# A two-layer decoder trunk: probabilities and last residual turned over by pass-through transposes, rows normalized first, tiles at multiples of 64 bytes

## The chip, the cores and the metric

The kernel runs on one core of a Trainium2 chip. The metric is the device time of one execution in microseconds (us). Every time below comes from the profile page of the kernel before, from queries to its trace, or from the list of its runs.

## What is computed

Batch 1, 512 tokens, model width 1024, two layers, float32 throughout. Layer 0 mixes tokens with a chunked gated MLP, layer 1 with forgetting attention; each is followed by a convolutional gated MLP (FFN), and a last RMSNorm ends the trunk. The part of the reference that the change touches is the softmax and its product with the values, and the last residual addition:

```python
logits = logits + cum[:, :, q0:q1, None] - cum[:, :, None, :q1]
logits = jnp.where(mask, logits, neg)
p = jax.nn.softmax(logits, axis=-1)
outs.append(jnp.einsum("bhqk,bkhd->bqhd", p.astype(vb.dtype), vb))
...
h = h + conv_gated_ffn(hn, ...)      # the last one, then
return rmsnorm(h, final_norm_g)
```

There are 16 heads of 64 features and four query blocks of 128 tokens; query block qi sees (qi + 1) * 128 keys.

## The kernel before, in words

All large products are made on TensorE from operands split into two float32r parts (hi and lo), as three products for one (`triple`, lines 164 to 169). Weights arrive as 176 units of 128x1024 (`raw`), are split by ScalarE (`whi`, line 112) and VectorE (`wlo`, line 113) and feed either `gemm_fm` (weights stationary, 512 tokens moving) or `gemm_tm` (tokens stationary, 512 weight columns moving). Activations that enter from a norm lie in tiles `x`; those that enter an output or down projection lie in tiles `z`. So the products with `z` are the gMLP's output projection (8 output tiles x 16 k tiles x 3 = 384 products of 512 columns), the first FFN's down projection (384), the attention's output projection (8 x 8 x 3 = 192) and the last down projection `last_down`, where `z` is the stationary side (7 token tiles of 512 columns over two groups x 16 x 3 = 336, and one tile in two halves of 256 columns, 96).

Where a tile lies is settled by the order in which its name is first asked for. The tile `mv` (line 227, statistics of the layer norm) takes 128 x (4 x 2) floats, 32 bytes of a partition. The tiles asked for before it and used on TensorE (`h`, `raw`, `whi`, `wlo`, `x`, `tmp`, `ident`, `v`) begin at multiples of 64 bytes; `R`, `pt`, `tc`, `z` and `hl`, asked for after it, begin 32 bytes beyond one.

The attention runs in slots of `attend` (line 518): a slot issues the sums of values of a block that is 7 slots old, then the transposes (`turn`) of one that is 5 slots old, then the logits of a new one. Blocks of the q and k projections (`qk`, two heads a time, 16 blocks of 3 products) are put between slots by a list written out by hand, `(4, 2, 2, 2, 2, 2, 1, 1)` blocks ahead of the 8 slots of two heads. For the last pair of heads, blocks of the output projection take their place. The engines run beside one another, each in an order fixed when the program is built.

`logits(h, qi)` makes two products into PSUM (lines 542 and 543) and adds the mask (544). VectorE takes the negated row maximum (546), ScalarE the exponentials with their sum into the head's tile `pr` (tag `pt`, line 547), VectorE the inverse of the sum (548), and then a 128x128 diagonal of the inverses in a tile `dg` (tag `tmp`, line 549). `turn(h, kb)` multiplies each 128x128 block of `pr`, as the stationary side, by the diagonal of its query block (line 559), which transposes and normalizes at once; there are 4 + 3 + 2 + 1 = 10 such products a head. They are plain float32 products, and the trace shows each as two records, a weight load and a matmul in both. The result is split (lines 112 and 113 into `hl`) and multiplied with the values (572 and 573).

`last_down` puts the residual into PSUM ahead of the down projection: 32 products of a 128x128 block of `h`, as the stationary side, with the identity (line 634), 16 ahead of each of the two groups.

Of the kernel before, what the change touches and what calls it, by code (L numbers as in the profile page):

```python
# [12 lines left out]
AF = mybir.ActivationFunctionType  # L13
ALU = mybir.AluOpType
# [3 lines left out]
T = 512            # tokens  # L18
D = 1024
KD = D // P        # feature tiles of the model width  # L20
E = 2048           # gMLP width and FFN width
KE = E // P
G = 8              # spatial groups
NT = T // P        # token tiles
H = 16             # heads
# [4 lines left out]
LAG = 7            # blocks between the logits and the sums of values  # L30

# columns of the packed per-feature vectors
V_MIX = 0          # mix_norm_g, 2 layers x 8 tiles
V_FFN = 16         # ffn_norm_g, 2 x 8
V_CW = 32          # conv taps, 2 x 3 x 16
V_CB = 128         # conv bias, 2 x 16
V_LG = 160         # ln_g, 16
V_LB = 176         # ln_b, 16
NV = 192
NU = 176           # units of weights  # L40


class Trunk:
# [41 lines left out]
    def unit(self):  # L85
        """The next unit of weights, in two parts; the one after it is under way."""
        while len(self.ahead) < 2 and self.iu < NU - 4:
            self.fetch()
        return self.ahead.pop(0)

# [1 line left out]
    def rsqrt(self, src, n, scale, eps):  # L92
        """[P, n] -> 1/sqrt(src*scale + eps): a first guess from the exponent, then Newton."""
        nc = self.nc
        ms, y, t = self.small(n), self.small(n), self.small(n)
        nc.vector.tensor_scalar(out=ms, in0=src, scalar1=scale, scalar2=eps, op0=ALU.mult, op1=ALU.add)
        nc.vector.tensor_scalar(out=y.bitcast(I32), in0=ms.bitcast(I32), scalar1=-0.5, scalar2=float(0x5F3759DF),
                                op0=ALU.mult, op1=ALU.add)
        for _ in range(3):
            self.newton(y, ms, t)  # L100
        return y

    def newton(self, y, ms, t):
        """y towards 1/sqrt(ms)."""
        nc = self.nc
        nc.vector.tensor_tensor(out=t, in0=y, in1=y, op=ALU.mult)
        nc.vector.scalar_tensor_tensor(out=t, in0=t, scalar=-0.5, in1=ms, op0=ALU.mult, op1=ALU.mult)
        nc.vector.scalar_tensor_tensor(out=y, in0=t, scalar=1.5, in1=y, op0=ALU.add, op1=ALU.mult)
# [6 lines left out]
    def norm_split(self, k, gcol, parts=1):  # L115
        """Operand parts of h*g for feature tile k."""
        nc = self.nc
        if k == 0:
            self.acc, self.xh, self.xl = None, [], []
        h = self.h[k]  # L120
        g = self.vec[:, gcol + k : gcol + k + 1]
        xh = self.sb("x", 16, [P, T], F32R)
        xl = self.sb("x", 16, [P, T], F32R)
        for q in range(parts):
            c = slice(q * T // parts, (q + 1) * T // parts)
            nc.scalar.activation(out=xh[:, c], in_=h[:, c], func=AF.Copy, scale=g)
            nc.vector.scalar_tensor_tensor(out=xl[:, c], in0=h[:, c], scalar=g, in1=xh[:, c].bitcast(F32),
                                           op0=ALU.mult, op1=ALU.subtract)
        self.xh.append(xh)
        self.xl.append(xl)  # L130

    def norm_square(self, k):
        """Feature tile k's share of the sum of squares."""
        nc = self.nc
        if self.acc is None:
            self.acc = self.tmp()
            nc.scalar.activation(out=self.acc, in_=self.h[k], func=AF.Square)
        else:
            sq = self.tmp()
            nc.scalar.activation(out=sq, in_=self.h[k], func=AF.Square)  # L140
            nc.gpsimd.tensor_tensor(out=self.acc, in0=self.acc, in1=sq, op=ALU.add)  # L141

    def norm_end(self):
        """r4[:, i]: 1/rms of token i*128+p.  R: the same along the free axis, on every partition."""
        nc = self.nc
        pt = self.ps("a")
        for i in range(NT):
            nc.tensor.matmul(pt[:, i : i + 1], self.acc[:, i * P : (i + 1) * P], self.ones[:, 0:1], start=True, stop=True)
        self.r4 = self.rsqrt(pt[:, 0:NT], NT, 1.0 / D, RMS_EPS)
        dg = self.tmp()  # L150
        for i in range(NT):
            nc.vector.tensor_scalar(out=dg[:, i * P : (i + 1) * P], in0=self.ident, scalar1=self.r4[:, i : i + 1],
                                    scalar2=None, op0=ALU.mult)
        self.dg = dg
# [9 lines left out]
    def triple(self, out, a, b, start, stop):  # L164
        """a*b to float32's accuracy from the exact parts of a and b."""
# [5 lines left out]
    def gemm_fm(self, o, nk, groups, evac, each=None, banks0=None):  # L171
        """Feature-major: four 128-feature tiles a group, weights stationary.  Yields after every 128x128 block."""
# [15 lines left out]
    def gemm_tm(self, o, nk, groups, evac, each=None):  # L188
        """Token-major: four token tiles a group of 512 features, tokens stationary."""
# [21 lines left out]
    def add_to_h(self, gcol):  # L211
        """Evacuation of an output product: the residual, then the next norm's operand."""
# [10 lines left out]
    def gmlp(self):  # L223
# [3 lines left out]
        mv = self.sb("mv", 1, [P, NT, 2])  # L227
# [38 lines left out]
        def mix(c):  # L266
            """The mixed chunks of feature tile c, with the norm's scale and shift and the spatial bias."""
# [42 lines left out]
    def spatial(self):  # L310
        """Causal spatial weights, transposed: [s, g, t], with their sums over s on every partition."""
# [46 lines left out]
    def fox(self):  # L358
# [4 lines left out]
        # the parts of the gates' weights side by side  # L363
# [44 lines left out]
        # Blocks of products fill the tensor engine's waits in the attention: logits of one head beside  # L408
        # the transposes and sums of the one before it.
# [20 lines left out]
    def gates(self):  # L430
        """Logs of the forget gates, [token, head]."""
# [14 lines left out]
        # log sigmoid z = min(z, 0) - log(1 + e^-|z|);  log(1 + e^-|z|) = 2 atanh s,  s = (1 - th)/(3 + th),  th = tanh(|z|/2)  # L446
# [15 lines left out]
    def running_sums(self):  # L462
        """Running sums of the logs, [head, token], in two parts, and negated: four rows a head beside the parts of
        q and of k: cum, cum, 1, 1 and 1, 1, -cum, -cum."""
# [29 lines left out]
    def stack_q(self, p, pq, st):  # L494
        """Operands of the logits of heads 2p and 2p+1: the parts of q and k, stacked along the contraction."""
# [22 lines left out]
    def attend(self, slot):  # L518
        """Logits of one block; some blocks behind them the transposes, and behind those the sums of values."""
# [9 lines left out]
    OFF = (0, 128, 384, 768)   # where the rows of a query block begin in a head's tile of probabilities  # L529

    def logits(self, h, qi):
        """Softmax's numerators of query block qi, and the diagonal of its normalizers' inverses."""
        nc = self.nc
        if qi == 0:
            self.pr[h] = (self.sb("pt", 3, [P, 1280]), self.tmp())
        pr, dg = self.pr[h]
# [10 lines left out]
        nc.scalar.activation(out=pr[:, self.OFF[qi] : self.OFF[qi] + w], in_=s[:, 0:w], func=AF.Exp, bias=nm, accum_out=sm)  # L547
        nc.vector.reciprocal(out=rc, in_=sm)
        nc.vector.tensor_scalar(out=dg[:, q], in0=self.ident, scalar1=rc, scalar2=None, op0=ALU.mult)

    def turn(self, h, kb):
        """Probabilities of key block kb, transposed and normalized, in two parts."""
        nc = self.nc
        pr, dg = self.pr[h]
        n = (NT - kb) * P
        pt = self.ps("a")
        for qi in range(kb, NT):
            o = self.OFF[qi] + kb * P
            nc.tensor.matmul(pt[:, (qi - kb) * P : (qi - kb + 1) * P], pr[:, o : o + P], dg[:, qi * P : (qi + 1) * P],  # L559
                             start=True, stop=True)  # L560
# [28 lines left out]
    def last_down(self):  # L589
        """Token-major down projection with the residual, then the final norm."""  # L590
# [13 lines left out]
        def finish(i, parts):  # L604
            # 1/rms from a square root and one step of Newton's
# [18 lines left out]
        for g in range(2):  # L624
            # a token tile's columns, in two parts where the norm of the last tile waits for them
# [4 lines left out]
            for i in range(NT):  # L630
                for bank, c in parts[i]:
                    for k in range(c.start // P, c.stop // P):
                        o = k * P - c.start
                        nc.tensor.matmul(bank[:, o : o + P], self.h[4 * g + k][:, i * P : (i + 1) * P], self.ident,  # L634
                                         start=o == 0, stop=False)
# [12 lines left out]
        # the last quarter token tile by token tile, so that only the last tile's norm is left at the end  # L648
# [16 lines left out]
    def build(self):  # L665
        nc, tc = self.nc, self.tc
        with tc.tile_pool(name="sb", bufs=1) as self.pool, \
# [3 lines left out]
            # the activation table and the tensor engine's clock get ready while the first loads run  # L671
# [64 lines left out]
def blocks(w):  # L736
    """[K, 512*n] -> units of two 128-row tiles by 512 columns, group by group."""
# [5 lines left out]
def qk_blocks(w):  # L743
    """q and k columns of a pair of heads beside each other, four 128-row tiles a unit."""
# [49 lines left out]
```

## Time and profile before

| what | us |
|---|---|
| runs: median of 3 (lowest to highest) | 1113.28 (1111.95 to 1115.22) |
| profiled execution: span, first to last instruction | 1110.7 |
| its own time beside the span | not listed apart; the fastest run is 1.25 above the span |
| TensorE matmul busy | 1098.0 (99%) |
| TensorE weight loads busy | 905.7 (82%) |
| VectorE busy | 618.5 (56%) |
| ScalarE busy | 443.5 (40%) |
| TensorE's granted clock, mean | 0.998 |

A matmul's duration in the trace is from its start until its modelled end; matmuls overlap, so the distance from one start to the next is what one costs TensorE. Busy times count overlapping instructions of an engine once. Idle time of an engine that does not set the end costs nothing.

### The profile page before, as it was taken

The numbers are of one execution on the slowest core, as the hardware profiler recorded it, in microseconds if no ns is written. First come the engines' busy times: TensorE is split into PE (matmuls) and PEld (weight loads), VectorE is DVE, ScalarE is ACT, GpSimd is POOL, SyncE is SP. The second block draws the span as 40 slices with busy tenths as digits, with TensorE's granted clock in tenths as the row PEclk, the third lists the DMA queues.
The fourth block names the chain that finished last, engine by engine and source line by source line (L and its number), as shares of the span: only waits on it lengthen the run. The fifth ranks groups of instructions, "written<-read, shape, count | busy, mean of one in ns | idle before, by whom it ended". The sixth has DMA issues, their size and how long they took to land. (4 is left out here: it accounts for less than half of the span.)

```text
span 1110.7 us, 13297 instructions
## 1 busy us (share of the span) xinstructions
PE 1098.0 (99%) x5210; PEld 905.7 (82%) x5210; DVE 618.5 (56%) x1007; ACT 443.5 (40%) x706; POOL 66.4 (6%) x62
## 2 busy tenths in 40 slices
PE   8999999999999999999999999999999999999997
PEld 6878888888888888888888788888878888888886
DVE  6435765533556655624264688888665656644232
ACT  5332333332334333423142566776542434332222
POOL 6000000000200000001020000000021000000000
PEclk9999999999999999999999999999999999999999
DMA  7322222223222222222222212111122222222222
GB/s 245 103 78 98 91 76 95 76 95 95 95 95 95 94 95 95 95 96 94 95 95 82 79 40 62 58 40 58 62 90 95 95 96 95 95 95 94 96 77 76
DMA packets 28959, 99.47 MB, mean 90 GB/s; under 512 B 3488, under 2 KB 4256, under 8 KB 28896
## 3 DMA queue, kind: packets, MB, share of 16 engines
q1 hardware_dynamic: 28752, 98.52, 26.9%
q8 instruction: 41, 0.67, 0.2%
q14 instruction: 22, 0.18, 0.1%
q10 hardware_dynamic: 144, 0.10, 0.0%
HBM read 96.12 MB, written 2.10 MB: 88 GB/s over the span
## 5 line engine op out<-in xcount | busy, mean ns | idle before, releaser
L113 DVE TENSOR_TENSOR wlo<-raw,whi 128x1024 fp32r<-128x1024 f32 (+1 forms) x173 | 218.8, 1266 | 389.8 <-ACT whi L112 377.4
L112 ACT CAST whi<-raw 128x1024 fp32r<-128x1024 f32 (+1 forms) x173 | 180.7, 1045 | 467.0 <-PE psg L168 124.2
L167 PE MATMUL psg<-x,whi 128*128 128x512 f32 x336 | 136.7, 407 | 0.0
L169 PE MATMUL psg<-x,wlo 128*128 128x512 f32 x336 | 131.3, 391 | 0.0
L168 PE MATMUL psg<-x,whi 128*128 128x512 f32 x336 | 130.8, 389 | 0.0
L167 PE MATMUL pss<-x,whi 128*128 128x512 f32 x208 | 81.9, 394 | 0.0
L169 PE MATMUL pss<-x,wlo 128*128 128x512 f32 x208 | 81.0, 390 | 0.0
L168 PE MATMUL pss<-x,whi 128*128 128x512 f32 x208 | 80.9, 389 | 0.0
L169 PEld LDWEIGHTS psg<-x,wlo 128*128 128x128 f32 x336 | 63.1, 188 | 13.8
L167 PEld LDWEIGHTS psg<-x,whi 128*128 128x128 f32 x336 | 63.9, 190 | 11.1 <-issue 0.2
L168 PEld LDWEIGHTS psg<-x,whi 128*128 128x128 f32 x336 | 63.3, 189 | 11.2 <-issue 0.2
L141 POOL TENSOR_TENSOR tmp<-tmp,tmp 128x512 f32<-128x512 f32 x28 | 46.3, 1655 | 408.4 <-ACT tmp L140 406.9
L167 PE MATMUL psg<-z,whi 128*128 128x512 f32 x128 | 51.1, 401 | 0.0
L168 PE MATMUL psg<-z,whi 128*128 128x512 f32 x128 | 50.6, 395 | 0.0
L169 PE MATMUL psg<-z,wlo 128*128 128x512 f32 x128 | 50.6, 395 | 0.0
L559 PE MATMUL psa<-tmp,pt 128*128 128x128 f32 x320 | 47.4, 278 | 0.2 <-DVE hl L113 0.2
L168 PEld LDWEIGHTS pss<-x,whi 128*128 128x128 f32 x208 | 39.1, 188 | 8.2 <-issue 0.2
L169 PEld LDWEIGHTS pss<-x,wlo 128*128 128x128 f32 x208 | 39.0, 188 | 8.2
L547 ACT ACTIVATE pt<-pss,sm 128x128 f32<-128x128 f32 (+1 forms) x64 | 33.7, 527 | 30.1 <-DVE sm L546 29.7
L167 PEld LDWEIGHTS pss<-x,whi 128*128 128x128 f32 x208 | 39.1, 188 | 8.1 <-issue 0.2
L559 PEld LDWEIGHTS psa<-tmp,pt 128*128 128x128 f32 x320 | 43.1, 191 | 2.9 <-DVE hl L113 1.3
L167 PE MATMUL psa<-x,whi 128*128 128x512 f32 x112 | 44.2, 394 | 0.0
(283 smaller groups left out, 2279.2 us busy)
## 6 DMA issues: line engine op xcount, KB each, us to landing
raw<-w SPq DMA_DIRECT2D x175, 512.0 KB
out<-v SPq DMA_DIRECT2D x8, 256.0 KB
h<-x SPq DMA_DIRECT2D x3, 512.0 KB
raw<-w SPq DMA_DIRECT2D x2, 256.0 KB
h<-x SPq DMA_DIRECT2D x4, 128.0 KB
pt<-ws SPq DMA_DIRECT2D x1, 512.0 KB
pt<-bs SPq DMA_DIRECT2D x1, 512.0 KB
z<-cum SPq DMA_DIRECT2D x32, 8.0 KB
```

The costliest lines, as they stand in the source:

```text
L112: nc.scalar.copy(out=hi, in_=src)
L113: nc.vector.tensor_tensor(out=lo, in0=src, in1=hi.bitcast(F32), op=ALU.subtract)
L141: nc.gpsimd.tensor_tensor(out=self.acc, in0=self.acc, in1=sq, op=ALU.add)
L167: self.nc.tensor.matmul(out, ah, bh, start=start, stop=False)
L168: self.nc.tensor.matmul(out, ah, bl, start=False, stop=False)
L169: self.nc.tensor.matmul(out, al, bh, start=False, stop=stop)
L547: nc.scalar.activation(out=pr[:, self.OFF[qi] : self.OFF[qi] + w], in_=s[:, 0:w], func=AF.Exp, bias=nm, accum_out=sm)
L559: nc.tensor.matmul(pt[:, (qi - kb) * P : (qi - kb + 1) * P], pr[:, o : o + P], dg[:, qi * P : (qi + 1) * P], start=True, stop=True)
```

## The change

Four edits. `logits` no longer makes a diagonal; it multiplies the row of `pr` in place by the inverse of its sum, 128 to 512 columns. `turn` transposes each block with `nc.tensor.transpose` (the data pass through TensorE, the identity is the moving side). `last_down` marks its 32 products with the identity as transposes. `mv` is asked for with 64 bytes of a partition, of which half is used, so that all later tiles move by 32 bytes. All other lines of the diff take out comments.

```diff
-        mv = self.sb("mv", 1, [P, NT, 2])
+        mv = self.sb("mv", 1, [P, NT, 4])[:, :, 0:2]
...
         if qi == 0:
-            self.pr[h] = (self.sb("pt", 3, [P, 1280]), self.tmp())
-        pr, dg = self.pr[h]
+            self.pr[h] = self.sb("pt", 3, [P, 1280])
+        pr = self.pr[h]
...
-        nc.scalar.activation(out=pr[:, self.OFF[qi] : self.OFF[qi] + w], in_=s[:, 0:w], func=AF.Exp, bias=nm, accum_out=sm)
+        row = pr[:, self.OFF[qi] : self.OFF[qi] + w]
+        nc.scalar.activation(out=row, in_=s[:, 0:w], func=AF.Exp, bias=nm, accum_out=sm)
         nc.vector.reciprocal(out=rc, in_=sm)
-        nc.vector.tensor_scalar(out=dg[:, q], in0=self.ident, scalar1=rc, scalar2=None, op0=ALU.mult)
+        nc.vector.tensor_scalar(out=row, in0=row, scalar1=rc, scalar2=None, op0=ALU.mult)
...
-        pr, dg = self.pr[h]
+        pr = self.pr[h]
...
-            nc.tensor.matmul(pt[:, (qi - kb) * P : (qi - kb + 1) * P], pr[:, o : o + P], dg[:, qi * P : (qi + 1) * P],
-                             start=True, stop=True)
+            nc.tensor.transpose(pt[:, (qi - kb) * P : (qi - kb + 1) * P], pr[:, o : o + P], self.ident)
...
                         nc.tensor.matmul(bank[:, o : o + P], self.h[4 * g + k][:, i * P : (i + 1) * P], self.ident,
-                                         start=o == 0, stop=False)
+                                         start=o == 0, stop=False, is_transpose=True)
```

## Rows read from the trace of the kernel before

**Rows 1.** The page's first part: busy us (share of span), instructions.
```profile
PE 1098.0 (99%) x5210; PEld 905.7 (82%) x5210; DVE 618.5 (56%) x1007; ACT 443.5 (40%) x706; POOL 66.4 (6%) x62
```

**Rows 2.** TensorE's waits, whole run: its longest, and the one at the transposes.
```profile
PE psg L168 <- DVE wlo L113: 2.3, 2, 1.4
...
PE psa L559 <- DVE hl L113: 0.2, 1, 0.2
```

**Rows 3.** Windows of one pair of heads each: first and last of six.
```profile
core 0: us, PE busy (x) PEld busy (x) DVE busy (x) ACT busy (x) POOL busy (x), PEclk, DMA share, GB/s
640.00:661.54 21.54, 21.54 (x130) 18.38 (x129) 17.93 (x44) 14.94 (x35) 1.67 (x2) 1.00 0.17 51
...
747.70:769.24 21.54, 21.54 (x130) 18.36 (x129) 18.01 (x45) 15.24 (x36) 1.23 (x2) 1.00 0.15 49
```

**Rows 4.** Windows in products of `z` moving, `x` moving, `z` stationary; columns as above.
```profile
210.00:280.00 70.00, 70.00 (x302) 56.22 (x301) 23.06 (x21) 17.18 (x20) 5.33 (x3) 1.00 0.29 96
320.00:460.00 140.00, 140.00 (x619) 115.96 (x618) 82.77 (x107) 53.68 (x67) 0.00 (x0) 1.00 0.29 95
...
1022.00:1054.00 32.00, 32.00 (x139) 25.77 (x138) 8.21 (x8) 7.69 (x10) 0.00 (x0) 1.00 0.28 85
```

**Rows 5.** TensorE's timeline, residual of the last projection: start, us, instruction, records merged.
```profile
1007.20 1.05 PE L634 MATMUL psa<-ident,h 128*128 128x128 f32 x8
1008.09 1.06 PE L634 MATMUL psb<-ident,h 128*128 128x128 f32 x8
1008.98 0.39 PE L634 MATMUL psg<-ident,h 128*128 128x128 f32 x2
```

**Rows 6.** Groups by line: the transposing products of the attention; records, busy us, mean ns.
```profile
L559 PE MATMUL psa<-tmp,pt 128*128 128x128 f32 x320 | 47.4, 278 | 0.2 <-DVE hl L113 0.2
```

**Rows 7.** TensorE's timeline: float32 products that move one column, and their neighbours.
```profile
847.36 0.39 PE L169 MATMUL psb<-x,wlo 128*128 128x512 f32 x1
847.59 0.95 PE L148 MATMUL psa<-ones,tmp 128*128 128x1 f32 x8
848.39 0.49 PE L167 MATMUL pss<-x,whi 128*128 128x512 f32 x1
848.72 0.40 PE L168 MATMUL pss<-x,whi 128*128 128x512 f32 x1
```

**Rows 8.** TensorE's timeline: two float32r products that move 128 columns.
```profile
801.45 0.22 PE L572 MATMUL psb<-hl,v 128*128 128x128 f32 x1
801.50 0.30 PE L573 MATMUL psb<-hl,v 128*128 128x128 f32 x1
801.64 0.44 PE L167 MATMUL psg<-z,whi 128*128 128x512 f32 x1
```

**Rows 9.** VectorE's groups by form: scaling 128 columns by one scalar; 512 by two.
```profile
L549 DVE TENSOR_SCALAR tmp<-ident,sm 128x128 f32<-128x128 f32 x64 | 18.9, 295 | 1.5
L259 DVE TENSOR_SCALAR v<-v,mv,sm 128x512 f32<-128x512 f32 x16 | 7.6, 538 | 0.0
```

**Rows 10.** VectorE's waits from 640 to 770 us: us in total, times, longest.
```profile
DVE sm L548 <- ACT pt L547: 7.9, 13, 0.7
DVE wlo L113 <- ACT whi L112: 4.5, 6, 0.7
```

**Rows 11.** Timelines: a head's last diagonal on VectorE, then its first transposes on TensorE.
```profile
665.59 0.28 DVE L549 TENSOR_SCALAR tmp<-ident,sm 128x128 f32<-128x128 f32 x1
...
666.31 1.06 PE L559 MATMUL psa<-tmp,pt 128*128 128x128 f32 x8
```

**Rows 12.** Groups by form: products of 512 columns with `x` and with `z`.
```profile
L168 PE MATMUL psg<-x,whi 128*128 128x512 f32 x336 | 130.8, 389 | 0.0
...
L168 PE MATMUL psg<-z,whi 128*128 128x512 f32 x128 | 50.6, 395 | 0.0
```

**Rows 13.** ScalarE's exponentials: the group over all forms, and reading out the sums.
```profile
L547 ACT ACTIVATE pt<-pss,sm 128x128 f32<-128x128 f32 (+1 forms) x64 | 33.7, 527 | 30.1 <-DVE sm L546 29.7
...
L547 ACT ACTIVATION_READ_ACCUMULATOR pt<-pss,sm 128x1 f32 x64 | 12.3, 193 | 0.0
```

## The prediction, made before the changed kernel ran

> **What bounds the kernel now.** First the page's busy shares: TensorE works in 99% of the span, VectorE in 56%, ScalarE in 40% [rows 1]. A high share may still hide waits, so next the list of waits: in the whole run TensorE's longest entry is 2.3 us, and at the transposes it waits 0.2 us in all [rows 2]. So TensorE's own work sets the time in every stage, and what leaves TensorE leaves the span, as long as nothing else is late in its place. The place to look for that is the attention. There a window of one pair of heads (two heads, 8 slots) repeats every 21.54 us; TensorE fills it, VectorE works 18.0 of it, ScalarE 15.2 [rows 3]. Only here is a second engine near the bound; in the stages of large products VectorE works 33% (23.06 of 70 us) to 59% (82.77 of 140) [rows 4]. Gains elsewhere can be taken whole, gains here only until VectorE is full.
>
> Durations are those of the profiled execution, whose span is 1110.7 us; the median of the runs, 1113.3, is 2.6 above it (0.2%). I take my sum off the median, as what lies around the span stays.
>
> **Last residual.** Sixteen records follow one another at 8.98 - 7.20 = 1.78 us, 0.111 us each [rows 5]. A product with the identity is two records, 0.223 us. What a pass-through transpose costs is not in the trace. Low end: 0.05 us, the distance between two single-record products of 128 columns [rows 8]. High end: 0.223, if it still runs as two records; nothing makes it less than one pass over the same columns, and a price above is a rival below. The nearest row is that of products which move a single column: eight records in 0.80 us, with a late next matmul (0.33 instead of 0.23) 0.90, so 0.11 a record with next to nothing to move [rows 7]. That is the price of loading a float32 block of 128 columns as weights, and a transpose still loads one. I take one record, 0.111 us. So 32 x 0.111 = **3.6 us** gained (0 to 32 x 0.17 = 5.4). TensorE alone is busy here; nothing covers or eats the gain.
>
> [...]
>
> **Turning the probabilities.** 320 records of the same kind [rows 6] are 160 products, 20 a pair of heads. On TensorE a pair loses 20 x 0.111 = 2.2 us: 21.54 becomes 19.3. VectorE gets more to do. Line 549 costs 295 ns for 128 columns now; 512 columns by two scalars cost 538 [rows 9]. Straight between them, rows of 128, 256, 384 and 512 cost 295, 376, 457 and 538 ns, 0.49 us a head more, 0.97 a pair. VectorE then needs 18.0 + 0.97 = 18.97 us of a pair that TensorE could do in 19.3. It is in order and waits for ScalarE now, 7.9 us for exponentials and 4.5 for weight parts in the 6 pairs from 640 to 770 us, 2.1 a pair [rows 10]. If all of that stayed, a pair would last 21.1 us; if none, 19.3. A fuller VectorE has other work in hand when an exponential is late, so I take a value nearer the TensorE end, 20.1 us. What is late next is the last row of a head: its diagonal is done at 665.87 and the head's transposes begin at 666.31 [rows 11]. The 0.24 us that the row of 512 costs more fits into these 0.44 today, but not with certainty when TensorE comes 10% earlier; behind the waiting transpose stand the logits and projections of the slot. That is why I don't take 19.3.
>
> Seven pairs of 20 make 140 of the 160 transposes. Gain 7 x (21.54 - 20.1) = 10.1 us. The last 20 run beside the output projection with little for VectorE to do: 20 x 0.111 = 2.2. Together **12.3 us**. Bounds: with pairs of 21.1, 3.1 + 2.2 = 5.3; with transposes of 0.05 us TensorE would need 21.54 - 3.4 = 18.1 and VectorE's 18.97 would bind, 7 x 2.57 + 20 x 0.17 = 21.4. The diagonal's tile is no longer held; no wait for a `tmp` tile stands among the waits, so that counts nothing. ScalarE and the queues of DMAs get no instruction more or less.
>
> **Tiles at multiples of 64 bytes.** The matmuls with `x` last 389 ns, those with `z` 395 [rows 12]. What each costs is seen in windows: 302 matmuls touch 70 us of products that move `z`, 139 touch 32 us in which `z` is stationary, 619 touch 140 us of products that move `x` [rows 4]. As a matmul of 0.39 us is counted in both windows at an edge, I take off 1.7: 0.2331, 0.2331 and 0.2268 us. All are at full clock, with the same 128 weight columns and 512 moving columns. `x`, `whi` and `wlo` lie at multiples of 64 bytes, `z` 32 beyond; whichever side `z` is on, the product costs 6.3 ns more. After the change `z` lies as `x` does. 384 + 384 + 192 + 336 = 1296 products of 512 columns with `z`: 1296 x 0.0063 = **8.2 us**. Bounds: 0, if the place matters for another reason; 9, if the 96 half-wide products gain as well. A loss is excluded as far as the trace tells, since the tiles move to where the faster ones are. The logits, values and `pt` blocks move too; a few ns on some 32 products a pair lie within the bounds.
>
> **Sum.** 12.3 + 3.6 + 8.2 = 24.1 us. 1113.3 - 24.1 = **1089 us** (2.2%; span 1086.6).
>
> **Rivals.**
> A: the place of `z` is not the cause. For it: 16 `z` tiles lie in another part of the memory than `x`, and no row separates the place from the remainder by 64. Against: 6.3 ns with `z` on either side, in stages with idle and with busy VectorE. Then 24.1 - 8.2 = 15.9: 1097 us. [...]
> B: VectorE holds the pairs at 21.1 us, as all its waits for ScalarE stay. Gain 5.3 + 3.6 + 8.2 = 17.1: 1096 us.
> C: the change doesn't do what it says: a float32 transpose still takes two records of 0.111 us. VectorE's 18.97 hides in 21.54, and only the 8.2 remain: 1105 us; with A as well 1113, no change.
> D, slower: the order of VectorE puts each inverse right behind its row maximum, so that it stands through every exponential. Eight a pair, 527 + 193 ns each [rows 13], 5.8 us: 18.97 + 5.8 = 24.7 us a pair. That costs 7 x 3.2 = 22.4 against 2.2 + 3.6 + 8.2 = 14.0 gained elsewhere: 1122 us. It decides from pairs of 21.54 + (14.0 + 3.3) / 7 = 24.0 us on. Against: now VectorE does other work between the two, and waits there 13 times in 48 exponentials [rows 10].
> [...]
>
> **Chances.** The forecast has 0.59, A 0.15, B 0.13, C 0.05, C with A 0.03, D 0.04, E 0.01. About 0.3% (3.3 us) is what a measurement of this kernel can tell from no change. Faster: 0.59 + 0.15 + 0.13 + 0.05 = 0.92; same 0.03; slower 0.05. The forecast's own fast end, with transposes of 0.05 us, is 21.4 + 5.4 + 9 = 35.8 gained, 1077.5; the range begins at 1078. It reaches up past A and B to half of the step to C, 1102, and so leaves out C, D and E, 0.13, and a little of A with B.
>
> **What would show it.** Right: 160 and 32 records of transposes instead of 320 and 64, 0.11 us apart; windows of a pair of about 20 us with VectorE over 90% busy in them; matmuls with `z` 0.227 us apart, 389 ns long; on VectorE line 549 at 295 to 540 ns by its width. Wrong: 320 records (C); `z` still at 0.233 (A); TensorE waiting for line 549 or VectorE for line 547 in each slot (B, D); a granted clock under 1.00 in the attention (E). Should the transposes stand 0.05 us apart, the load was no bound and the time lies at the range's low end.

## The result, and the profile after

| | before | after |
|---|---|---|
| median of the runs (lowest to highest), us | 1114.03 (1111.95 to 1115.22) | 1095.47 (1093.93 to 1096.86) |
| span of the profiled execution, us | 1110.7 | 1093.4 |

There are four runs of each here, one more of before than stood ahead of the prediction. The ratio is 0.9837, 95% interval [0.9822, 0.9852]: 18.6 us faster, where 24.1 were forecast. Lines of `logits` and `turn` stand one further down in the new kernel: exponential 548, inverse 549, scaling of the row 550, transposes 560.

The page's first part, as [rows 1]. TensorE issues 192 records less, 160 of the turn and 32 of the residual; that is one record a transpose instead of two.

```profile
PE 1075.3 (98%) x5018; PEld 882.4 (81%) x5018; DVE 620.2 (57%) x1007; ACT 440.7 (40%) x706; POOL 67.3 (6%) x62
```

TensorE's waits of the whole run, as [rows 2]: us in total, times, longest. The second and third are new.

```profile
PE psg L168 <- DVE wlo L113: 3.3, 2, 2.4
PE psa L560 <- DVE pt L550: 2.6, 5, 0.5
PE psa L167 <- ACT whi L112: 1.4, 1, 1.4
```

Where the 17.3 us of the two spans lie is read from the first and the last product of logits, and from the first product of the last residual. First the kernel before, then the one after (minimum, median and maximum in ns, then the first and the last start in us):

```profile
L542 PE MATMUL pss<-z,z x64: 223/364/480, 624.4 to 790.9; 128*128 128x128 f32 x16, 128*128 128x256 f32 x16, 128*128 128x384 f32 x16, 128*128 128x512 f32 x16
```

```profile
L542 PE MATMUL pss<-z,z x64: 221/388/477, 621.9 to 777.8; 128*128 128x128 f32 x16, 128*128 128x256 f32 x16, 128*128 128x384 f32 x16, 128*128 128x512 f32 x16
```

| stretch, us | before | after | gain |
|---|---|---|---|
| start to the first logits | 624.4 | 621.9 | 2.5 |
| first logits to the last | 166.5 | 155.9 | 10.6 |
| last logits to the last residual (1007.20, 994.02) | 216.3 | 216.2 | 0.1 |
| last residual to the end | 103.5 | 99.4 | 4.1 |

**Last residual.** TensorE's timeline of the new kernel, as [rows 5]: start, us, instruction, records merged.

```profile
994.02 0.60 PE L634 MATMUL psa<-ident,h 128*128 128x128 f32 x4
994.46 0.60 PE L634 MATMUL psb<-ident,h 128*128 128x128 f32 x4
994.89 1.04 PE L634 MATMUL psg<-ident,h 128*128 128x128 f32 x8
995.68 0.48 PE L167 MATMUL psa<-whi,z 128*128 128x512 f32 x1
```

Eight transposes from 994.02 to 994.89 are 0.109 us each, one record a transpose. The 16 of this group end at 995.68, after 1.66 us; before they took from 1007.20 to 1010.69, 3.49. Two groups save 3.7 us of TensorE.

**Pairs of heads.** Window of one of them, as [rows 3], same columns: 20.29 us instead of 21.54, at a granted clock of 1.00. TensorE is idle 0.5 us in it, and VectorE works 18.2 of it.

```profile
658.74:679.03 20.29, 19.77 (x110) 15.99 (x109) 18.17 (x44) 14.91 (x36) 1.56 (x2) 1.00 0.17 55
```

**Products with `z`.** Windows in the stages of [rows 4], same columns: `z` moving, `x` moving, and 28 us with `z` stationary.

```profile
210.00:280.00 70.00, 70.00 (x308) 57.43 (x307) 23.69 (x21) 17.22 (x21) 5.26 (x3) 1.00 0.28 98
320.00:460.00 140.00, 140.00 (x619) 115.98 (x618) 81.82 (x105) 53.67 (x67) 0.00 (x0) 1.00 0.28 95
1000.00:1028.00 28.00, 28.00 (x122) 22.56 (x121) 6.12 (x5) 5.25 (x5) 0.00 (x0) 1.00 0.28 98
```

With 1.7 taken off each count, as in the prediction: `z` moving costs 70 / 306.3 = 228.5 ns (before 233.1), `x` moving 226.8 as before, `z` stationary 28 / 120.3 = 233 ns, as before (233.1). So after the change a product is cheaper where `z` moves, by 4.6 of the 6.3 ns, and not at all where it is stationary.

### The profile page after: what moved, and what is told of

Same layout as the page of the kernel before. It is cut to its first block, busy times and chain, and to the rows that moved or that the text cites. A ratio compares the mean times of both kernels' runs of the same rounds, so it can differ in the third digit from the quotient of the medians.

```text
span 1093.4 us, 12918 instructions
## 1 busy us (share of the span) xinstructions
PE 1075.3 (98%) x5018; PEld 882.4 (81%) x5018; DVE 620.2 (57%) x1007; ACT 440.7 (40%) x706; POOL 67.3 (6%) x62
## 5 line engine op out<-in xcount | busy, mean ns | idle before, releaser
L167 PE MATMUL psa<-x,whi 128*128 128x512 f32 x112 | 44.1, 394 | 0.0
L169 PE MATMUL psb<-x,wlo 128*128 128x512 f32 x112 | 43.6, 389 | 0.0
L168 PE MATMUL psa<-x,whi 128*128 128x512 f32 x112 | 43.6, 389 | 0.0
L167 PE MATMUL psb<-x,whi 128*128 128x512 f32 x112 | 43.6, 389 | 0.0
```

Source lines behind the costliest of these rows:

```text
L167: self.nc.tensor.matmul(out, ah, bh, start=start, stop=False)
L168: self.nc.tensor.matmul(out, ah, bl, start=False, stop=False)
L169: self.nc.tensor.matmul(out, al, bh, start=False, stop=stop)
```

## What the transposes wait for

The timeline of the new kernel around one of its waits at line 560 (all engines; in brackets the idle time before an instruction and what ended it):

```profile
660.45 1.23 DVE L113 TENSOR_TENSOR wlo<-raw,whi 128x1024 fp32r<-128x1024 f32 x1
660.45 0.69 ACT L548 ACTIVATE pt<-pss,sm 128x512 f32<-128x512 f32 x1 [1.06 <-DVE sm L546]
...
660.81 0.49 PE L560 MATMUL psa<-ident,pt 128*128 128x128 f32 x3
661.04 0.19 ACT L548 ACTIVATION_READ_ACCUMULATOR pt<-pss,sm 128x1 f32 x1
...
661.59 0.15 DVE L549 RECIPROCAL sm<-sm 128x1 f32<-128x1 f32 x1
...
661.63 0.23 PE L544 MATMUL pss<-maskb,identb 128*128 128x128 bf16 x1
661.66 0.27 DVE L113 TENSOR_TENSOR hl<-psa,hl 128x128 fp32r<-128x128 f32 x1
...
661.85 0.48 DVE L550 TENSOR_SCALAR pt<-pt,sm 128x512 f32<-128x512 f32 x1
...
662.38 0.33 PE L560 MATMUL psa<-ident,pt 128*128 128x128 f32 x1 [0.52 <-DVE pt L550]
```

Three blocks of the head's first key block are turned at once; the fourth is in the row of 512, the head's last. Its exponentials are done at 661.14 and its sum at 661.23, but VectorE is in a part of weights until 661.68, then does the inverse, a small split and the scaling, which ends at 662.33. The transpose starts 0.05 us later. So the row is late because of what stands ahead of it on VectorE, not because of ScalarE.

VectorE's groups by form for the scaling, 640 to 770 us, where [rows 9] have the diagonals:

```profile
L550 DVE TENSOR_SCALAR pt<-pt,sm 128x512 f32<-128x512 f32 x13 | 7.4, 568 | 0.0
...
L550 DVE TENSOR_SCALAR pt<-pt,sm 128x384 f32<-128x384 f32 x13 | 5.3, 410 | 0.0
...
L550 DVE TENSOR_SCALAR pt<-pt,sm 128x256 f32<-128x256 f32 x13 | 4.5, 344 | 0.2
...
L550 DVE TENSOR_SCALAR pt<-pt,sm 128x128 f32<-128x128 f32 x13 | 3.6, 277 | 0.0
```

## Experiments

Each run stands beside new runs of the kernel before, whose medians were 1113.0 to 1113.3 us. Edits are against the changed kernel unless another is named.

### Whose doing the faster z is: its place or its distance

The start of a tile in a partition is taken from the compiled program; no row here shows it. `whi` and `x` start at multiples of 512 bytes; `z` starts at 149280 before (32 beyond a multiple of 256) and at 149312 after (64 beyond). The sizes of the tiles, added up in the order of their first use with each in whole steps of 32 bytes, agree: from `whi` to `z` they make 117536 bytes before and 117568 after, also 32 and 64 beyond a multiple of 256. First the edit of `mv` was undone:

```diff
-        mv = self.sb("mv", 1, [P, NT, 4])[:, :, 0:2]
+        mv = self.sb("mv", 1, [P, NT, 2])
```

> The changed kernel with `mv` back at 32 bytes: only the transposes and the scaled rows are left of the change. Theory P (the place in the memory, by its remainder, sets the cost of a product): products that move `z` go back from 0.2288 to 0.2333 us, 960 x 0.0045 = 4.3 us, about 1100 us against 1095.5; products with `z` stationary stay at 0.233. Theory Q (the faster products with `z` come from something else in the change, such as the order of the work): no change, 1095.5 us and 0.2288 us.

1100.75 us, ratio 0.9891 [0.9874, 0.9907]. Windows, `z` moving and `z` stationary:

```profile
210.00:280.00 70.00, 70.00 (x302) 56.22 (x301) 23.31 (x21) 17.18 (x20) 5.33 (x3) 1.00 0.29 94
...
1010.00:1038.00 28.00, 28.00 (x122) 22.55 (x121) 6.13 (x5) 5.26 (x5) 0.00 (x0) 1.00 0.30 95
```

302 products again where `z` moves, and no change where it is stationary. The place is a cause. The edit is worth 5.3 us by the medians; by the spans 3.6 (1097.0 and 1093.4), and 4.5 if the start is set aside, where this run waits 0.95 us less. Then `mv` got 128 bytes, so that `z` lies at 128 beyond a multiple of 256:

```diff
+        mv = self.sb("mv", 1, [P, NT, 8])[:, :, 0:2]
```

> The changed kernel with `mv` of 128 bytes, so that `R`, `pt`, `z` and `hl` begin at multiples of 128 bytes, as `x`, `whi` and `wlo` do, and not 64 beyond one. Theory P128 (the remainder by 128 counts): products with `z` cost what those with `x` cost, 0.2267 us, moving (888 outside the attention's slots x 0.0021 = 1.9 us) and stationary (336 x 0.0066 = 2.2 us), about 1091.4 us. Theory P64 (only the remainder by 64 counts, the remaining difference is the part of the memory in which `z` lies): nothing changes, 1095.5 us, 0.2288 and 0.233 us.

1099.43 us, 0.9877 [0.9862, 0.9891]: slower than the changed kernel by 4.0.

```profile
210.00:280.00 70.00, 70.00 (x303) 56.76 (x302) 24.11 (x22) 18.18 (x21) 5.32 (x3) 1.00 0.29 92
```

303 products, 232.3 ns each: a rounder address made it slower, and both theories missed the time. Next, a tile of 64 bytes ahead of `x` moved `x`, `tmp`, `ident`, `v` and all behind them by 64, `whi` not:

```diff
+            nc.gpsimd.memset(self.sb("pad", 1, [P, 16]), 0.0)
```

> The changed kernel with a tile of 64 bytes ahead of `x`: `x`, `tmp`, `ident` and `v` now begin 64 bytes beyond a multiple of 128, and `z`, `pt` and `hl` at a multiple. Theory P128: the two kinds swap. Products that move `x` go from 0.2267 to about 0.2288 us (1920 outside the attention x 0.0021 = 4.0 us), those with `x` stationary to 0.233 (576 x 0.0066 = 3.8 us), those with `z` to 0.2267 (4.1 us less): about 1099 us. Theory P64: no change, 1095.5 us, `x` at 0.2267 and `z` at 0.2288.

1106.81 us, 0.9941 [0.9927, 0.9956]. Windows, `z` moving (now 128 beyond) and `x` moving (now 64 beyond):

```profile
210.00:280.00 70.00, 70.00 (x303) 56.74 (x302) 25.58 (x26) 17.81 (x22) 5.31 (x3) 1.00 0.31 98
320.00:460.00 140.00, 140.00 (x612) 114.54 (x611) 84.95 (x110) 55.82 (x70) 0.00 (x0) 1.00 0.30 94
```

612 products with `x` instead of 619: 229.4 ns, what `z` costs at 64 beyond. The time is above both expected ones. So `x` is not fast in itself; what counts lies between the two operands or in each address. The next two runs tell these apart. In the first, `z` alone moves on, to 149504, a multiple of 256:

```diff
+        mv = self.sb("mv", 1, [P, NT, 16])[:, :, 0:2]
```

> The changed kernel with `mv` of 256 bytes: `z`, `pt` and `hl` begin at a multiple of 512 bytes, as `whi`, `wlo` and `x` do. After e2 and e3 the remainder of a tile alone no longer explains the costs: `z` at a multiple of 128 costs more (0.2329) than at 64 beyond one (0.2289). Theory D (what counts is the distance of the two operands' starts, by its remainder by 256: 0 gives 0.2268 us, 64 gives 0.2289 with the moving side ahead, 32, 128, 192 and 224 give 0.2326 to 0.2334): the distance is 0 here, all products with `z` take 0.2268 us, 888 x 0.0021 + 336 x 0.0065 = 4.0 us less than the changed kernel, about 1091.5 us. Theory G (the part of the memory in which `z` lies costs): no better than the changed kernel's 0.2289, 1095.5 us or more.

1093.55 us, 0.9816 [0.98, 0.9832].

```profile
210.00:280.00 70.00, 70.00 (x311) 57.98 (x310) 24.56 (x23) 18.25 (x21) 5.21 (x3) 1.00 0.30 96
...
1000.00:1028.00 28.00, 28.00 (x125) 23.18 (x124) 6.14 (x6) 5.27 (x5) 0.00 (x0) 1.00 0.32 107
```

311 products: 226.3 ns, as `x`; and for the first time `z` as the stationary side gains too, 125 in 28 us instead of 122, 227 ns. In the second, weights, `x` and `z` all move by 64, so that addresses change and distances don't:

```diff
-            self.vec = self.sb("vec", 1, [P, NV])
+            self.vec = self.sb("vec", 1, [P, NV + 16])[:, 0:NV]
```

> The changed kernel with 64 bytes more ahead of `raw`, so that `whi`, `wlo`, `x`, `tmp`, `ident` and `v` all begin 64 bytes beyond a multiple of 128, and `z` at a multiple. Theory D: the distance of `x` from `whi` is still 0, 0.2268 us; `z` is 64 from `whi` as in the changed kernel, 0.2289 moving and 0.2333 stationary: 1095.5 us in all. Theory A (each operand's own remainder counts, 0 being the good one for `x`): products that move `x` stay at 0.2289 or more and those with `x` stationary at 0.233, as in e3, 1107 us or more.

1095.8 us, 0.9838 [0.9819, 0.9857], the changed kernel's time.

```profile
210.00:280.00 70.00, 70.00 (x307) 57.42 (x307) 22.45 (x20) 18.25 (x21) 5.24 (x3) 1.00 0.29 98
320.00:460.00 140.00, 140.00 (x619) 115.98 (x618) 80.43 (x103) 52.35 (x66) 0.00 (x0) 1.00 0.30 97
```

So it is the distance, as far as one shift of both operands by 64 bytes tells. By all runs, for the start of the moving operand less that of the stationary one, within 256 bytes (a negative distance counts from 256 downwards):

| distance | 0 | 64 | 128 | 32, 192, 224 |
|---|---|---|---|---|
| ns a product of 512 columns | 226 to 227 | 228.5 to 229.4 | 232.3 | 233 |

That the period isn't 128 is shown. Where the distance was 0, both tiles lay at multiples of 512, so 256 is not told apart from 512 there; but by the starts above, `z` in the changed kernel lies 320 from `whi` within 512 bytes and `x` in the run with the 64 bytes ahead of it lies 64, and both cost the same, which speaks for 256.

By these numbers the distance 0 should bring 960 x 2.2 + 336 x 6 ns = 4.1 us more than the change; the medians show 1.9, and the time lies between the two expected ones. The profile shows where most of the rest went. TensorE's timeline at the start, and a window of 10 us around it with its granted clock:

```profile
22.35 0.50 PE L168 MATMUL psg<-wlo,x 128*128 128x512 f32 x1 [2.44 <-DVE wlo L113]
...
23.01 0.63 PE L167 MATMUL psg<-whi,x 128*128 128x512 f32 x1
23.44 0.63 PE L168 MATMUL psg<-wlo,x 128*128 128x512 f32 x1
...
26.34 0.40 PE L168 MATMUL pss<-wlo,x 128*128 128x512 f32 x1
```

```profile
18.00:28.00 10.00, 7.56 (x27) 5.72 (x26) 5.53 (x4) 1.56 (x2) 7.74 (x7) 0.83 0.47 158
```

After the wait of 2.44 us the next ten products take 3.99 us; most of them stand 0.43 us apart instead of 0.23, and the granted clock of the window is 0.83. The changed kernel waits 2.39 us at the same place, its clock stays at 1.00, and its ten products take 2.41:

```profile
22.36 0.50 PE L168 MATMUL psg<-wlo,x 128*128 128x512 f32 x1 [2.39 <-DVE wlo L113]
...
24.77 0.39 PE L168 MATMUL pss<-wlo,x 128*128 128x512 f32 x1
```

```profile
18.00:28.00 10.00, 7.61 (x34) 5.98 (x33) 5.54 (x4) 1.89 (x3) 7.77 (x7) 1.00 0.43 133
```

So the lower clock cost this run 1.6 us, and the length of the wait alone doesn't decide whether it comes. In the profiles of this study the start comes in three ways: the wait is 1.44 us, with a granted clock of 1.00 from 18 to 28 us (before, and three of the runs), 2.4 with 1.00 (the changed kernel, and one run), or 2.3 to 2.4 with 0.83 (the other eight runs). That moves a span by 0.95 or some 2.6 us, whatever the experiment is about. One execution of each kernel was profiled, so how its other runs start isn't recorded. Why the wait is longer in some kernels was not tried.

### The last residual

Products with the identity again:

```diff
-                                         start=o == 0, stop=False, is_transpose=True)
+                                         start=o == 0, stop=False)
```

> The changed kernel with the last residual put in by products with the identity again, 64 records instead of 32. If the term of the prediction holds, 3.6 us more than the changed kernel, about 1099 us, with 16 products in 3.56 us instead of 1.75; if the gain was hidden by something that ends later, 1095.5 us.

1098.1 us, 0.9865 [0.9843, 0.9887]: 2.6 us above the changed kernel by the medians, 3.2 by the spans (1096.6 and 1093.4), for 3.7 of TensorE in the timeline. The intervals of the two ratios overlap a little, so the size of this one rests on the trace: from the last residual to the end this run takes 103.0 us where the changed kernel takes 99.4, which is the whole 3.6; its first logits come 0.5 us earlier.

### What the turn gains and what the scaled rows cost

First the turn by products with the identity, rows still normalized first:

```diff
-            nc.tensor.transpose(pt[:, (qi - kb) * P : (qi - kb + 1) * P], pr[:, o : o + P], self.ident)
+            nc.tensor.matmul(pt[:, (qi - kb) * P : (qi - kb + 1) * P], pr[:, o : o + P], self.ident, start=True, stop=True)
```

> The changed kernel with the turn of the probabilities made by products with the identity again (rows still normalized first, all else as in the changed kernel). If a pass-through transpose saves 0.109 to 0.111 us of TensorE on each of 160, and all of it is time but for the new wait of 0.5 us a pair: 320 records at line 560, pairs 20.29 + 2.2 less up to 0.5, so 21.5 to 22.3 us, and 160 x 0.11 = 17.6 less 7 x 0.5 at most: 1109 to 1113 us. If part of the gain at the transposes is given back elsewhere (the output projection's new wait of 1.35 us, the start), that wait is gone here and the time is 1107 to 1109.

1104.81 us, 0.9919 [0.9904, 0.9934]. Both expected sums missed. A window of a pair:

```profile
660.63:682.20 21.57, 21.57 (x132) 18.37 (x130) 18.80 (x44) 15.24 (x36) 1.23 (x2) 1.00 0.16 51
```

The pair is back at 21.57 us, TensorE fills it, and VectorE works 18.80 of it: 0.8 more than with the diagonals, hidden. By the medians the turn is worth 9.3 us, by the spans 9.5 (1102.9 and 1093.4), in the attention 11.0 (the first to the last logits take 166.9 us); 1.3 of that the start takes back, where this run has the shorter wait. What I left out of the sum is that this wait costs more than its idle time, as the next run shows. It drops the scaling:

```diff
-        nc.vector.tensor_scalar(out=row, in0=row, scalar1=rc, scalar2=None, op0=ALU.mult)
```

> The changed kernel without the scaling of the rows (line 550 is left out, so the probabilities enter the sums of values unnormalized; the inverse of the sum is still made and not used). Theory W (the 0.5 us that TensorE waits once a pair of heads is for the scaled row, and it is the whole of what the scaling costs): the wait at the transposes goes or names ScalarE's row and shrinks, a pair lasts 19.8 instead of 20.29, attention about 3.5 us shorter, 1092 us. Theory V (VectorE's load as a whole spreads the pair, by late parts of weights and late row maxima too): without 0.42 us a head of work on VectorE the pair falls below 19.6, 1090 or less. Theory N (what waits is the head's last exponential, not the scaling behind it): the wait stays at 0.4 to 0.5 and the time at 1095.

1089.86 us, 0.9781 [0.9763, 0.9799]. A window of a pair:

```profile
659.81:679.28 19.47, 19.47 (x111) 15.88 (x109) 15.94 (x36) 15.15 (x36) 1.57 (x2) 1.00 0.18 57
```

The pair takes 19.47 us and TensorE no longer waits. So the scaling costs 0.82 us a pair, not the 0.52 that stand as a wait. The timeline of the last section shows why: the late transpose starts 0.75 us after the product ahead of it (661.63 to 662.38), where one of this kind is otherwise followed after some 0.05; the idle time counts only from that product's modelled end. So the size is theory V's, but most of the loss sits at the scaled row, as in W. By the medians the scaling costs 5.6 us, by the spans 4.9 (1088.6 and 1093.4): 4.6 between the first and the last logits (151.3 us), where five of the pairs wait for the row; 1.6 behind them, where a wait of the output projection for weights (1.4 us in the changed kernel) goes as well; and the start takes 1.3 back. The 160 transposes alone, this run against the last, are worth 14.95 us by the medians and 14.4 by the spans; the start hides 2.7 of that (the first logits come at 623.2 us here, at 620.5 there), so that 17.1 to 17.6 are left, as 160 x 0.11 makes.

Next, a lag of 8 slots instead of 7, with all the work left in:

```diff
-LAG = 7
+LAG = 8
```

> The changed kernel with the transposes and the sums of values one slot later (LAG 8). Theory L (TensorE's 0.5 us of idle time a pair of heads is the latency of one scaled row, which is late for its transpose): the idle time goes, a pair lasts 19.6 to 19.8 instead of 20.29 us, 7 x 0.6 = 4 us less, about 1091.5 us. Theory V (VectorE is full): the wait stays in another place, a pair lasts 20.2 to 20.4 us, 1095 to 1097 us.

1094.25 us, 0.9831 [0.9816, 0.9846]. Window of a pair:

```profile
678.81:698.78 19.97, 19.70 (x112) 15.93 (x110) 18.20 (x44) 14.59 (x36) 1.23 (x2) 1.00 0.17 55
```

and among TensorE's waits:

```profile
PE psb L573 <- DVE hl L113: 1.1, 4, 0.3
```

The wait for the scaled row is gone, and the next one on VectorE, for the split of the turned blocks, holds the pair at 19.97, between what the two theories had. The first to the last logits take 2.3 us less, but 1.3 of that is the work of one slot that now stands behind the last logits (from there to the last residual it is 217.5 instead of 216.2 us), and the start (granted clock 0.83 from 18 to 28 us) takes 1.2: by the spans nothing is gained (1093.5 and 1093.4), by the medians 1.2. Together with `mv` of 256 bytes:

> Both together: distance 0 and the transposes one slot later. If the gains add, 4.0 us from the places and the 1.2 us that e4 showed: about 1090.3 us, with pairs of heads of 19.9 us. If the output projection's wait for weight parts (1.35 us in the changed kernel) and the sums' waits take the second gain back, 1091.5 us.

1092.22 us, 0.9802 [0.9783, 0.982], above both expected times. The pair is the same:

```profile
677.56:697.54 19.98, 19.71 (x112) 15.92 (x110) 18.20 (x44) 14.61 (x36) 1.23 (x2) 1.00 0.17 55
```

If the rest is VectorE's load, giving one row of four to another engine must end it. Against this last version, ScalarE got the row of 512:

```diff
+        if qi == NT - 1:
+            nc.scalar.activation(out=row, in_=row, func=AF.Copy, scale=rc)
+        else:
+            nc.vector.tensor_scalar(out=row, in0=row, scalar1=rc, scalar2=None, op0=ALU.mult)
```

> The version with distance 256 and a lag of 8 slots, and the last row of each head (512 columns) scaled by ScalarE instead of VectorE. That takes about 0.57 us a head from VectorE, the engine that is fullest in a pair, and gives ScalarE, which works 15 of 20 us, about as much. If VectorE's load as a whole holds the pairs at 19.95: pairs of 19.5, the attention 3 us shorter, 1089 us. If the order of ScalarE matters more (the scaling stands behind the inverse, which waits for ScalarE's own exponential; the copies and splits queued behind it come later): the pairs stay at 19.9 or grow, with TensorE waiting for ScalarE at the transposes or for parts of weights, 1092 to 1096.

1088.22 us, 0.9778 [0.9762, 0.9794].

```profile
678.00:697.30 19.30, 19.30 (x111) 15.90 (x110) 17.05 (x42) 15.83 (x38) 1.22 (x2) 1.00 0.18 57
```

Or GpSimd got the row of 128:

```diff
+        eng = nc.gpsimd if qi == 0 else nc.vector
+        eng.tensor_scalar(out=row, in0=row, scalar1=rc, scalar2=None, op0=ALU.mult)
```

> The version with distance 256 and a lag of 8 slots, and the first row of each head (128 columns) scaled by GpSimd instead of VectorE: 0.28 us a head less on VectorE, on the row that the transposes need latest relative to its making least. If VectorE's load as a whole holds the pairs: half of what the last row on ScalarE brings, pairs of 19.7, 1090.5 us. If GpSimd is slow for it but has idle time (it works 1.5 us of a pair), nothing waits for it, since the first row is three slots ahead of the transposes; if it disturbs VectorE while it works, the pair stays at 19.95 or grows, 1092 or more.

1087.94 us, 0.9774 [0.976, 0.9789].

```profile
677.15:696.45 19.30, 19.30 (x111) 15.90 (x110) 17.65 (x42) 14.42 (x36) 2.42 (x4) 1.00 0.18 57
```

Both give pairs of 19.30 us in which TensorE never waits: the whole of the 20 x 0.111 us. Even 0.28 us a head was enough, more than I had expected of it. These two are not told apart from each other; both beat the kernel before by 2.2% and the changed one, which has neither the longer lag nor the distance 0, by 7 us. The row of 128 moved from VectorE to GpSimd took 4.3 us off the version with that lag and that distance (1092.22 and 1087.94).

## Why the prediction was right, and where its sizes were off

**The bound.** Right. TensorE set the time in every stage, and what left it left the span, except in the pairs, where VectorE was the second bound as named, and at the new waits below.

**Last residual, 3.6 us.** Right: one record of 0.109 us, 3.7 in the timeline. That agrees with the 0.11 taken as the price of loading the block as weights; that the load is what bounds it was not tried.

**Turning the probabilities, 12.3 us.** The mechanism was right, and the size is 9.3 by the medians, 11.0 in the attention, both against rows that are scaled already. The terms: a product loses 0.11 us, as taken. The pair lasts 20.29 us, where 20.1 was taken between 19.3 and 21.1. Its low end was seen: 19.30 is reached when VectorE is relieved. What holds the pair is the step that was named as "late next", the last row of a head: I doubted that 0.24 us more on it fit into 0.44, and TensorE waits 0.52 for it. The forecast lost 17.8 - 12.3 = 5.5 us to VectorE, 0.8 in each of seven pairs; the scaling costs 5.6 by the medians. That these agree so closely is in part luck: 4.6 lie in the attention, where only five pairs wait, and the rest is the output projection's new wait less what the start takes back. The price of the scaled rows was right as well (0.97 a pair taken, 0.8 in the run without transposes). But that price is no share of a sum: the durations of VectorE's instructions in a pair add up to 19.9 us before and 20.7 after, and its busy time rose only from 18.0 to 18.2, since they overlap at their ends when work is queued (the inverse at 661.59 lasts 0.15, and the next starts 0.07 after it). Rival B's 21.1 us fell for this reason more than for its own. VectorE's waits for ScalarE from 640 to 770 us, as [rows 10], shrank for exponentials and parts of weights, as expected, but a new one stands ahead of them, for ScalarE's part of the turned blocks:

```profile
DVE hl L113 <- ACT hl L112: 6.1, 7, 0.9
DVE sm L549 <- ACT pt L548: 2.4, 6, 0.4
DVE wlo L113 <- ACT whi L112: 2.1, 6, 0.7
```

**Tiles at multiples of 64 bytes, 8.2 us.** The step that failed. The sentence "After the change `z` lies as `x` does" took the remainder by 64 for the cause; it is the distance of the two operands. As distances, `x` had 0 and `z` went from 32 to 64 where it moves (960 x 4.6 ns = 4.4 us) and from 224 to 192 where it is stationary (nothing). By the medians of the runs the edit is worth 5.3. The bound "a loss is excluded" was also wrong in its reason: `z` at a multiple of 128 gained next to nothing (232.3 ns), and `x` moved by 64 bytes lost. The trace of before left this open: it showed 6.3 ns with `z` on either side, always against a tile at another remainder, and I read that as a property of `z`.

**New waits.** Not foreseen: the output projection now waits 1.4 us for a part of weights (ScalarE's group `whi`), which eats most of what the faster `z` and the last transposes bring there, and the start waits 0.95 us longer. The stretches of the first table show both: up to the first logits 768 x 4.6 ns = 3.5 us less 0.95 is the 2.5 found, and between the last logits and the residual 192 x 4.6 ns = 0.9 and eleven transposes' 1.2, less 1.4, leave 0.7, of which 0.1 was found; the difference is not accounted for.

**Rivals.** A fell: the place is the cause, by the run with `mv` back at 32 bytes. The measured 1095.47 lies near its 1097 all the same, since the stationary half gained nothing and other terms came out smaller. C fell: one record. D fell: six waits for an exponential from 640 to 770 us, not one in each slot. E, a granted clock under 1.00 in the attention, did not come: it is 1.00 in the pairs. A transpose there lasts 277 ns on the mean, one of the last residual 272, and the latter follow one another at 0.109 us.

## What to carry to other kernels

A float32 block is turned over by a pass-through transpose in half of TensorE's time of a product with the identity (0.109 us instead of 0.218 in the last residual), with one load and one product on record instead of two of each (5018 instead of 5210 in all); but the scaling that a diagonal did for nothing goes to another engine, and its last row is what the first transposes wait for. When a freed engine then waits in small pieces for a nearly full one, moving one instruction of 0.3 us a head off the full engine gave more (4.3 us) than a longer lag (1.2 to 1.3). Where two operands of a long series of products lie relative to each other is worth a look: here 3% of a product's time.

## What the runs showed of the hardware that was not expected

- The distance of the moving and the stationary operand, within 256 bytes (or 512), sets a product of 512 columns between 226 and 233 ns; moving both operands by 64 bytes left the products with `x` at 619 in 140 us.
- VectorE's instructions with two tensors as input lasted about twice as long (1.58 us each instead of 0.74) while GpSimd worked on two tensors. From the changed kernel's timeline:

```profile
795.58 0.74 DVE L127 SCALAR_TENSOR_TENSOR x<-h,vec,x 128x512 fp32r<-128x512 f32 x1
...
796.41 4.68 POOL L141 TENSOR_TENSOR tmp<-tmp,tmp 128x512 f32<-128x512 f32 x3 [36.97 <-ACT tmp L140]
...
796.91 4.73 DVE L127 SCALAR_TENSOR_TENSOR x<-h,vec,x 128x512 fp32r<-128x512 f32 x3
```

  One takes 0.74 us alone, three beside GpSimd 4.73. What the two engines wait for there was not tried. The scaling of a row of 512, with one tensor as input, lasted longer beside GpSimd too. Of the changed kernel's 16, the nine with no GpSimd instruction beside them last 475 to 485 ns (one stands at 661.85 above), the seven beside a copy of GpSimd 671 to 773; the mean of 568 mixes both. One of the seven:

```profile
650.24 0.61 POOL L504 CAST z<-tmp 64x512 fp32r<-64x512 f32 x1 [12.49 <-DVE tmp L498]
...
650.46 0.68 DVE L550 TENSOR_SCALAR pt<-pt,sm 128x512 f32<-128x512 f32 x1
```

  Where GpSimd took the row of 128, its scalings of 0.60 us never ran beside VectorE's scaling of a row, so that run doesn't show what the two would cost each other.

- After waits of nearly equal length (2.39 and 2.44 us) TensorE's granted clock from 18 to 28 us was 1.00 in one profiled execution and 0.83 in another, whose products stood 0.43 us apart from 23.01 to 26.00.
